# A transformer block with split fp32 products: which engine adds the output projection's results, and when the heads' sums are rounded

## The chip, the cores and the metric

The kernel runs on one core of a Trainium2 chip. A core has TensorE (PE, matrix products, results in PSUM), VectorE (DVE), ScalarE (ACT), GpSimd (POOL) and SyncE (SP, which issues most transfers). Each works through its own queue in order; semaphores order the engines among themselves. In this kernel POOL works on SBUF alone; a product's result that it adds is copied from PSUM to SBUF first. The metric is the time of one execution on the device in microseconds.

## The reference

One block of a hybrid model on 512 tokens of width 1024, all in fp32:

```
n = rmsnorm(x);  proj = n @ w_in
y_gla = gated linear attention, 4 heads, forward and backward
y_mla = softmax attention with latent q and kv, 8 heads, 512 x 512 scores each
merged = sigmoid(z_ma) * y_gla + sigmoid(z_mb) * y_mla
h = x + merged @ w_out
h = h + square(relu(rmsnorm(h) @ w_ff1)) @ w_ff2
out = rmsnorm(h)
```

The change touches the stretch from the softmax attention over `merged @ w_out` to the normalisation in front of the MLP.

## The kernel before

**Split products.** An fp32 operand is kept as two tiles, a rounded high part and the remainder. ACT writes the high part (`split`, line 93) and another engine, VectorE if nothing else is said, subtracts it from the source (line 94). A product is three matmuls: high by high, low by high, high by low (`mm3`, lines 88 to 90).

**Seven products.** The large products with 1024 x 1024 weights are cut into 2 x 2 blocks and done with seven block products in place of eight, on sums and differences of blocks. The left operand of products 1 and 2 are first blocks of `merged` themselves (`split_first`), of 5, 6, 7 and 3 sums of its blocks (`merged_sums` makes the tiles y and z, `split_sum` splits them), of 4 the last block (`corner`). The right operand comes from four weight blocks B11, B12, B21, B22. `load_w2` loads one by four transfers that SP issues; `load_onto` adds another block onto it in SBUF by two accumulating transfers from POOL's queue; `add_w2` adds on VectorE; `split_part` splits one half of a block (tiles bo50h, bo50l for product 5, half 0), `split_w2` both. The split halves share four buffers, so a half can be split when the half four before it has been used.

**The attention loop** (line 1244) runs 38 steps. Step n makes the scores of one head and 128 queries (`att_scores`: product, row maximum on VectorE, exponential on ACT, scaling on ACT or VectorE in turn), transposes those of step n - 3 (`att_flip`, split by ACT and VectorE) and, in every second step, multiplies two steps' probabilities by the values, six steps late (`att_values`). When a head is done, VectorE gates it and POOL adds it to the other branch (`merge`, line 1055). Two heads make a pair p of `merged`. At the end of the steps 13, 21 and 29 the sums of pairs 0, 1 and 2 are made on POOL (lines 928 to 931) and split at once: ACT rounds, POOL takes the remainder. The loop also holds the output weights' loads (steps 26 and 30), the splits of products 1 and 2 (28 and 31), and the first blocks of pairs 0 and 1 (26). In this loop a planner sets the order on ACT, VectorE and TensorE, from the order of the text as priority and from dependencies; POOL follows the text (line 1531). `goes_behind` adds an edge: the first instruction of one stretch behind the last of another on the same engine.

**The projection** (lines 1454 to 1530) runs the products in the order 1, 2, 5, 6, 3, 7, 4, on TensorE, ACT and VectorE in the order of the text (line 1530). Products 1, 6, 7 and 4 accumulate on top of each other in two PSUM banks (`xs_`), 5 and 3 in two others (`zs_`); what is in a bank after one product must be added to the residual rows before the next product goes on. `add_rows` does that on VectorE from PSUM; `add_rows_by_copy` copies on ACT (line 1293) and adds on POOL (line 1295). `normed` squares, scales and so normalises a row block, and `flipped` transposes it on TensorE and splits it for the MLP. Products 3, 7 and 4 run row block by row block.

Of the kernel before, what the change touches and what calls it, by code (L numbers as in the profile page):

```python
# [14 lines left out]
AF = mybir.ActivationFunctionType  # L15
ALU = mybir.AluOpType
# [3 lines left out]
S = 512  # L20
# [36 lines left out]
def tile_block(ctx: ExitStack, tc: tile.TileContext, t, out: bass.AP):  # L57
    nc = tc.nc
# [9 lines left out]
    def u2(name, dt=F32, shape=(P, S)):  # L68
        return tl(list(shape), dt, "u2", 29, name)
# [37 lines left out]
    def traced():  # L107
        return len(nc.cur_bb.bb.instructions)
# [810 lines left out]
    def split_w2(x, name):  # L919
        return [split_part(x, g, name) for g in range(NP // 2)]  # L920
# [24 lines left out]
    def up_units(pr):  # L945

        wq = stage(3, P, f"wq{pr}")
        for k in range(3):
            nc.sync.dma_start(
                wq[:, k, :].rearrange("p (h e) -> p h e", h=2), w_uq[:, k, 2 * pr : 2 * pr + 2, 0:NOPE]  # L950
            )
        wqh, wql = halves(3, P, f"wq{pr}")
        split(wqh, wql, wq, nc.gpsimd)
        wk = stage(2, 384, f"wk{pr}")
        nc.sync.dma_start(
            wk.rearrange("p k (h e) -> p k h e", h=2), w_ukv[:, :, 2 * pr : 2 * pr + 2, :]
        )
        wh, wl = halves(2, 384, f"wk{pr}")
        src = wk.rearrange("p k (h e) -> p k h e", h=2)
        for k in range(2):  # L960
            for c, e in ((slice(0, 128), slice(0, NOPE)), (slice(128, 384), slice(NOPE, 192))):
                split(wh[:, k, c].rearrange("p (h e) -> p h e", h=2),
                      wl[:, k, c].rearrange("p (h e) -> p h e", h=2), src[:, k, :, e], nc.gpsimd)
        qs = []
        for i in range(2):
            q = u4(f"q{pr}{i}")
            h = (2 * pr + i) * HALF
            for x in range(2):
                at = NOPE + x * HALF
                nc.sync.dma_start(raw(q[at : at + HALF]), raw(ro[x][h : h + HALF]))  # L970
            qs.append(q)
        yield
        accq = up_T(wqh, wql, cq, f"uq{pr}")
        for i in range(2):
            split_scaled(qs[i][0:64, 0, :], qs[i][0:64, 1, :], accq[i * 64 : i * 64 + 64, :], QK_SCALE)
        yield
        acck = up_T(wh[:, :, 0:128], wl[:, :, 0:128], ckv, f"uk{pr}")
        for i in range(2):
            kb = kbuf[2 * (pr % 2) + i]
            split(kb[0:64, 0, :], kb[0:64, 1, :], acck[i * 64 : i * 64 + 64, :])  # L980
        yield
        vs = []
        for j in range(2):
            acc = ps("mm", f"uv{pr}{j}")
            for i in range(2):
                tok = slice((2 * j + i) * P, (2 * j + i + 1) * P)
                for k in range(2):
                    mm3(acc[:, i * 256 : i * 256 + 256], ckv[k][:, 0, tok], ckv[k][:, 1, tok],
                        wh[:, k, 128:384], wl[:, k, 128:384], k == 0, k == 1)
            hl = u4(f"v{pr}{j}", F32R, (P, 2, 2, 256))  # L990
            flat = [hl[:, x].rearrange("p a b -> p (a b)") for x in range(2)]
            split_scaled(*flat, acc, 0.5)
            vs.append(hl)
            yield
        for i in range(2):
            heads[2 * pr + i] = (qs[i], kbuf[2 * (pr % 2) + i], vs, slice(i * MV, (i + 1) * MV))
# [244 lines left out]
    LAG_B, LAG_C = 3, 6  # L1241
    units = iter(())
    attending = traced()
    for n in range(4 * MH + LAG_C):
        if n % 8 == 1 and n // 8 + 1 < MH // 2:
            units = up_units(n // 8 + 1)
        if n < 4 * MH:
            att_scores(n // 4, n % 4)
        next(units, None)
        b = n - LAG_B  # L1250
        if 0 <= b < 4 * MH:
            flips = traced()
            att_flip(b // 4, b % 4)
            if b == 0:
                gla_turn(GH - 1, (flips, traced()))
        if n == 26:
            load_w2(0, B11, w_out)
            load_w2(0, B21, w_out)
            for p in range(2):
                split_first(wo_left[p], merged[p][0], f"o{p}", nc.gpsimd)  # L1260
        if n == 28:
            wo_right[1] = split_w2(B11, "bo1")
        if n == 29:
            load_onto(B11, B12, w_out)
        c = n - LAG_C
        if c >= 0 and c % 2 == 1:
            att_values(c // 4, (c % 4) // 2)
        if c > 0 and c % 8 == 7 and c // 8 < NP - 1:
            p = c // 8
            y, z = merged_sums(p, nc.gpsimd)  # L1270
            split_sum(wo_left[p], y, 5, 6, f"bo{p}", nc.gpsimd)
            split_sum(wo_left[p], z, 7, 3, f"co{p}", nc.gpsimd)
        if n == 30:
            load_w2(0, B12, w_out)
            load_w2(0, B22, w_out)
        if n == 31:
            wo_right[2] = split_w2(B21, "bo2")

    hrow = []
    for i in range(NT):  # L1280
# [6 lines left out]
    def add_rows(i, c, acc, op=ALU.add):  # L1287
        hc = hrow[i][:, c * S : (c + 1) * S]
        nc.vector.tensor_tensor(hc, hc, acc, op=op)  # L1289

    def add_rows_by_copy(i, c, acc, sign=1.0):
        part = u2(f"part{i}{c}")
        nc.scalar.activation(part, acc, AF.Copy, scale=sign)
        hc = hrow[i][:, c * S : (c + 1) * S]
        nc.gpsimd.tensor_tensor(hc, hc, part, op=ALU.add)

    ms_rows = {}

# [172 lines left out]
    split_first(wo_left[2], merged[2][0], "o2", nc.vector)  # L1471
    g_last = split_first(wo_left[last], merged[last][0], f"o{last}", nc.vector, None, slice(0, HT))
    wo_product(1)
    split_first(wo_left[last], merged[last][0], f"o{last}", nc.vector, g_last, slice(HT, S))
    wo_right[5] = [split_part(B11, 0, "bo5")]
    y, z = merged_sums(last, nc.vector)
    split_sum(wo_left[last], y, 5, 6, f"bo{last}")
    for rb in range(2):
        add_rows_by_copy(rb, 0, xs_[rb])
    load_onto(B12, B22, w_out)  # L1480
    wo_right[5].append(split_part(B11, 1, "bo5"))
    wo_product(2)
    add_w2(B11, B22, B11, ALU.add)
    for rb in range(2):
        add_rows(rb, 0, ws_[rb])
        first_half_square(rb, 0)
    wo_right[6] = split_w2(B11, "bo6")
    load_onto(B11, B21, w_out)
    load_w2(0, B21)
    wo_product(5)  # L1490
    split_sum(wo_left[last], z, 7, 3, f"co{last}")
    for rb in range(2):
        add_rows_by_copy(2 + rb, 1, zs_[rb])
    wo_right[3] = split_w2(B22, "bo3")
    load_w2(0, B22)
    for p in range(NP):
        corner(p, nc.gpsimd if p < last else nc.vector)
    wo_product(6)
    fm = Flipped(gvec[:, V_MLP : V_MLP + 8], "m")
    mT = fm.out  # L1500
    for rb in range(2):
        add_rows_by_copy(rb, 1, xs_[rb], -1.0)
    wo_right[7] = split_w2(B12, "bo7")
    load_w2(0, B12)
    for rb in range(2):
        wo_product(3, (rb,))
        add_rows(rb, 1, zs_[rb])
        normed(rb, 1)
    wo_right[4] = split_w2(B11, "bo4")
    load_w2(0, B11)  # L1510
    early = [proj_begin(w1, 0, "f00", "at")]
    for rb in range(2):
# [92 lines left out]
```

## Time and profile before

| | |
|---|---|
| median of 3 runs | 790.49 us (789.77 to 790.68) |
| profiled execution | 790.3 us, span 788.6 us |
| TensorE busy | 759.9 us |
| VectorE busy | 587.2 us |
| ScalarE busy | 456.4 us |
| GpSimd busy | 157.2 us |
| mean granted TensorE clock | 0.989 |

Times in the views count from the span's start. A timeline row has the start, the time taken, the engine, the line, the operation, the tile written and those read, the shape, the number of instructions, and in brackets how long the engine had stood idle before and what released it. A row of waits has the sum, the number of times and the longest. In a table of windows the clock that TensorE was granted stands as PEclk (1.00 is full).

### The profile page before, as it was taken

Reading aid. Unit: us, or ns where it says so; the run is one execution under the profiler, and the core shown is the slowest. Engines: PE = TensorE matmul, PEld = TensorE weight load, DVE = VectorE, ACT = ScalarE, POOL = GpSimd, SP = SyncE. Lnnn points to the kernel's source line nnn. Section 1 sums busy time; section 2 is a strip of 40 time slices with the busy share of each in tenths; the row PEclk is TensorE's granted clock in tenths of the full one; section 3 lists DMA queues with packets and bytes.
Section 4 is the critical chain, followed back from the end, with each engine's and each line's share of the span. In section 5 each row is a group of like instructions: output and inputs, shape, how many; then the busy total and the mean of one; then the engine's idle time right before and its main releaser. Section 6 shows DMA issues by size and latency. Waiting matters only on the chain.

```text
span 788.6 us, 10218 instructions
## 1 busy us (share of the span) xinstructions
PE 759.9 (96%) x3744; PEld 641.1 (81%) x3744; DVE 587.2 (74%) x857; ACT 456.4 (58%) x774; POOL 157.2 (20%) x233
## 2 busy tenths in 40 slices
PE   9999999999999999988697999999999999999996
PEld 7888788888888889877585888888888888888885
DVE  7688999576568676977768668875788487857695
ACT  8456666546485556876735676444653456436644
POOL 0710007062452032054734100000000000000014
PEclk9999999999999999999988999999999999999999
DMA  9734201132225233025637441055105511550002
GB/s 311 236 108 141 78 2 46 37 81 80 54 54 140 44 84 94 1 68 180 156 108 154 139 119 55 25 190 154 33 27 187 160 30 51 160 171 18 27 1 106
DMA packets 94945, 77.09 MB, mean 98 GB/s; under 512 B 15312, under 2 KB 74704, under 8 KB 94896
## 3 DMA queue, kind: packets, MB, share of 16 engines
q1 hardware_dynamic: 92752, 72.24, 31.1%
q0 software_dynamic: 1856, 3.93, 2.7%
q8 instruction: 29, 0.48, 0.3%
q10 hardware_dynamic: 288, 0.28, 0.1%
q14 instruction: 20, 0.16, 0.1%
HBM read 72.76 MB, written 2.10 MB: 95 GB/s over the span
## 4 chain that ended last, share of the span: by engine, by line
PE 84%; issue 5%; DVE 4%; POOL 3%; ACT 3%; POOLq 0%; DVEq 0%; ACTq 0%
PE f L89 7%; PE f L90 7%; PE f L88 7%; PE gx L88 4%; PE gx L90 4%; PE gx L89 4%; PE first L326 3%; PE za L88 2%; PE za L90 2%; PE za L89 2%; PE gz L88 2%; PE gz L90 2%; PE gz L89 2%; PE zb L88 1%; PE zb L90 1%
## 5 line engine op out<-in xcount | busy, mean ns | idle before, releaser
L1544 POOL DMA_DIRECT2D gfin<-in_g_final x1 | 0.6, 645 | 283.2 <-PE f L90 283.2
L912 DVE TENSOR_TENSOR w<-w,w 128x1024 f32<-128x1024 f32 x34 | 41.1, 1219 | 0.3
L474 POOL COPY v3f<-rrf 128x4 f32<-128x4 f32 x4 | 2.8, 708 | 135.8 <-DVE rrf L457 135.8
L1024 PE MATMUL tp<-ident,e 128*128 128x128 f32 x128 | 20.0, 283 | 7.4 <-ACT e L1015 5.7
L1024 PEld LDWEIGHTS tp<-ident,e 128*128 128x128 f32 x128 | 16.0, 145 | 10.6 <-ACT e L1015 5.9
L1010 ACT ACTIVATE e<-s,top 128x512 f32<-128x512 f32 x32 | 21.9, 684 | 3.9 <-DVE top L1007 3.7
L94 DVE TENSOR_TENSOR pT<-tp,pT 128x512 fp32r<-128x512 f32 x32 | 21.6, 682 | 1.9 <-ACT pT L93 1.8
L1289 DVE TENSOR_TENSOR h<-h,gx 128x512 f32<-128x512 f32 x32 | 21.5, 680 | 1.9 <-PE gx L90 1.8
L1007 DVE TENSOR_REDUCE top<-s 128x1 f32<-128x512 f32 x32 | 21.6, 679 | 1.1 <-PE s L90 1.0
L93 ACT ACTIVATE pT<-tp 128x512 fp32r<-128x512 f32 x32 | 18.8, 594 | 4.3 <-PE tp L1024 4.1
L88 PE MATMUL av<-pT,v 128*128 128x256 f32 x64 | 19.8, 309 | 0.0
L89 PE MATMUL av<-pT,v 128*128 128x256 f32 x64 | 19.1, 299 | 0.0
L90 PE MATMUL av<-pT,v 128*128 128x256 f32 x64 | 18.5, 290 | 0.0
L1367 ACT ACTIVATE fa<-f 128x512 f32<-128x512 f32 x32 | 18.5, 577 | 0.0
L88 PE MATMUL s<-kbuf,q 96*128 96x512 f32 x32 | 13.9, 434 | 4.7 <-ACT e L1010 4.7
L93 ACT ACTIVATE ghb<-y 128x512 fp32r<-128x512 f32 x16 | 10.1, 632 | 14.0 <-DVE y L859 14.0
L94 DVE TENSOR_TENSOR sc<-sc,sc 128x512 fp32r<-128x512 f32 x16 | 10.9, 690 | 9.5 <-ACT sc L93 9.5
L1055 POOL TENSOR_TENSOR mx<-tb,za 128x256 f32<-128x256 f32 x8 | 6.5, 816 | 50.0 <-DVE tb L1052 50.0
L93 ACT ACTIVATE sc<-sc 128x512 fp32r<-128x512 f32 x16 | 9.3, 595 | 11.5 <-DVE sc L545 11.5
L173 ACT ACTIVATE ms<-h 128x512 f32<-128x512 f32 x8 | 5.0, 628 | 18.7 <-DVE h L1289 18.7
L93 ACT ACTIVATE b_00h<-w 128x1024 fp32r<-128x1024 f32 x7 | 7.4, 1060 | 12.6 <-PE gz L90 6.0
L93 ACT ACTIVATE b_10h<-w 128x1024 fp32r<-128x1024 f32 x7 | 7.4, 1060 | 12.1 <-PE gz L90 6.0
(1643 smaller groups left out, 2961.2 us busy)
## 6 DMA issues: line engine op xcount, KB each, us to landing
w<-in_w_ff SPq DMA_DIRECT2D x64, 256.0 KB, 3.5
grw<-in_w_in SPq DMA_DIRECT2D x8, 512.0 KB, 9.2
gvw<-in_w_in SPq DMA_DIRECT2D x8, 512.0 KB, 4.7
w<-in_w_out SPq DMA_DIRECT2D x16, 256.0 KB, 3.6
w<-in_w_out POOLq DMA_DIRECT2D x6, 512.0 KB, 6.8
x<-in_xt SPq DMA_DIRECT2D x8, 256.0 KB, 5.2
vw<-in_w_first SPq DMA_DIRECT2D x8, 256.0 KB, 5.3
h<-in_x SPq DMA_DIRECT2D x4, 512.0 KB, 7.5
```

Of the source, the lines that this page charges most:

```text
L88: nc.tensor.matmul(acc, lh, rh, start=start, stop=False, skip_group_check=onto)
L89: nc.tensor.matmul(acc, lh, rl, start=False, stop=False, skip_group_check=onto)
L90: nc.tensor.matmul(acc, ll, rh, start=False, stop=stop, skip_group_check=onto)
L93: nc.scalar.activation(hi, src, AF.Copy)
L94: rest.tensor_tensor(lo, src, raw(hi), op=ALU.subtract)
L326: nc.tensor.matmul(f_accs[i], a[:, i * P : (i + 1) * P], b, start=k == 0 and x == 0, stop=k == KD - 1 and x == 2)
L912: nc.vector.tensor_tensor(wq[dst][g], wq[x][g], wq[y][g], op=op)
L1007: nc.vector.tensor_reduce(top, acc, axis=AX.X, op=ALU.max, negate=True)
L1010: nc.scalar.activation(e, acc, AF.Exp, bias=top, accum_out=tot)
L1024: nc.tensor.transpose(tp[:, k * P : (k + 1) * P], e[:, k * P : (k + 1) * P], ident)
L1289: nc.vector.tensor_tensor(hc, hc, acc, op=op)
L1367: nc.scalar.activation(a, acc, AF.Relu)
```

## The change

In the projection the six additions that went by ACT's copy and POOL become `add_rows` on VectorE, the second with a subtraction in place of a negated copy; the remainders of the last block for pairs 0, 1 and 2 go from POOL to VectorE. The splits of weight halves are put between these additions: half 0 of a block before them, half 1 behind; the halves of product 4 stand inside the loop over row blocks, each behind `normed`. The accumulating load of B22 onto B12 and the sum for product 6 come before the additions of product 1, and the split of the last pair's z before product 5.

In the attention loop the sums of pairs 0, 1 and 2 are made where they were, but split at steps 17, 25 and 31, and on ACT behind that step's scores. The first blocks of pairs 0 and 1 are split at step 25. The loads of B11 and B21 stand at step 20 (26 before), the splits of products 1 and 2 at 24 and 27 (28 and 31), the load of B12 onto B11 at 28 (29).

```diff
+    sums_of = {}
     for n in range(4 * MH + LAG_C):
...
+        scored = traced()
         if n < 4 * MH:
             att_scores(n // 4, n % 4)
+        scored = scored, traced()
...
-        if n == 26:
+
+        ready = traced()
+        if n in (17, 25, 31):
+            p = (n - 13) // 8
+            y, z = sums_of.pop(p)
+            split_sum(wo_left[p], y, 5, 6, f"bo{p}", nc.gpsimd)
+            split_sum(wo_left[p], z, 7, 3, f"co{p}", nc.gpsimd)
+            if p == 1:
+                for p in range(2):
+                    split_first(wo_left[p], merged[p][0], f"o{p}", nc.gpsimd)
+            goes_behind((ready, traced()), scored, SPLITTERS[:1])
+        if n == 20:
             load_w2(0, B11, w_out)
             load_w2(0, B21, w_out)
-            for p in range(2):
-                split_first(wo_left[p], merged[p][0], f"o{p}", nc.gpsimd)
+        if n == 24:
+            wo_right[1] = split_w2(B11, "bo1")
+        if n == 27:
+            wo_right[2] = split_w2(B21, "bo2")
         if n == 28:
-            wo_right[1] = split_w2(B11, "bo1")
-        if n == 29:
             load_onto(B11, B12, w_out)
+        if n == 30:
+            load_w2(0, B12, w_out)
+            load_w2(0, B22, w_out)
         c = n - LAG_C
         if c >= 0 and c % 2 == 1:
             att_values(c // 4, (c % 4) // 2)
         if c > 0 and c % 8 == 7 and c // 8 < NP - 1:
-            p = c // 8
-            y, z = merged_sums(p, nc.gpsimd)
-            split_sum(wo_left[p], y, 5, 6, f"bo{p}", nc.gpsimd)
-            split_sum(wo_left[p], z, 7, 3, f"co{p}", nc.gpsimd)
-        if n == 30:
-            load_w2(0, B12, w_out)
-            load_w2(0, B22, w_out)
-        if n == 31:
-            wo_right[2] = split_w2(B21, "bo2")
+            sums_of[c // 8] = merged_sums(c // 8, nc.gpsimd)
...
     wo_product(1)
+    wo_right[5] = [split_part(B11, 0, "bo5")]
     split_first(wo_left[last], merged[last][0], f"o{last}", nc.vector, g_last, slice(HT, S))
-    wo_right[5] = [split_part(B11, 0, "bo5")]
     y, z = merged_sums(last, nc.vector)
     split_sum(wo_left[last], y, 5, 6, f"bo{last}")
+    wo_right[5].append(split_part(B11, 1, "bo5"))
+    load_onto(B12, B22, w_out)
+    add_w2(B11, B22, B11, ALU.add)
     for rb in range(2):
-        add_rows_by_copy(rb, 0, xs_[rb])
-    load_onto(B12, B22, w_out)
-    wo_right[5].append(split_part(B11, 1, "bo5"))
+        add_rows(rb, 0, xs_[rb])
     wo_product(2)
-    add_w2(B11, B22, B11, ALU.add)
+    wo_right[6] = [split_part(B11, 0, "bo6")]
     for rb in range(2):
         add_rows(rb, 0, ws_[rb])
         first_half_square(rb, 0)
-    wo_right[6] = split_w2(B11, "bo6")
+    wo_right[6].append(split_part(B11, 1, "bo6"))
     load_onto(B11, B21, w_out)
     load_w2(0, B21)
+    split_sum(wo_left[last], z, 7, 3, f"co{last}")
     wo_product(5)
-    split_sum(wo_left[last], z, 7, 3, f"co{last}")
+    wo_right[3] = [split_part(B22, 0, "bo3")]
     for rb in range(2):
-        add_rows_by_copy(2 + rb, 1, zs_[rb])
-    wo_right[3] = split_w2(B22, "bo3")
+        add_rows(2 + rb, 1, zs_[rb])
+    wo_right[3].append(split_part(B22, 1, "bo3"))
     load_w2(0, B22)
     for p in range(NP):
-        corner(p, nc.gpsimd if p < last else nc.vector)
+        corner(p, nc.vector)
     wo_product(6)
...
+    wo_right[7] = [split_part(B12, 0, "bo7")]
     for rb in range(2):
-        add_rows_by_copy(rb, 1, xs_[rb], -1.0)
-    wo_right[7] = split_w2(B12, "bo7")
+        add_rows(rb, 1, xs_[rb], ALU.subtract)
+    wo_right[7].append(split_part(B12, 1, "bo7"))
     load_w2(0, B12)
     for rb in range(2):
         wo_product(3, (rb,))
         add_rows(rb, 1, zs_[rb])
         normed(rb, 1)
-    wo_right[4] = split_w2(B11, "bo4")
+        wo_right.setdefault(4, []).append(split_part(B11, rb, "bo4"))
```

More of the change, by code (lines that the diff above doesn't have):

```diff
@@ L1289, in add_rows @@
         nc.vector.tensor_tensor(hc, hc, acc, op=op)
[L1291 to L1295, printed above, removed]
     ms_rows = {}
```

## The prediction

> **What bounds the kernel now.** I read the page first, then TensorE's waits, then a table of windows over the second half of the attention and the projection (the stages that the change touches), and last the timeline of each engine around the waits.
>
> ```profile
> span 788.6 us, 10218 instructions
> PE 759.9 (96%) x3744; PEld 641.1 (81%) x3744; DVE 587.2 (74%) x857; ACT 456.4 (58%) x774; POOL 157.2 (20%) x233
> ```
> ```profile
> PE tp L1024 <- ACT e L1015: 5.7, 1, 5.7
> PE woz L89 <- DVE bo30l L94: 5.1, 1, 5.1
> PE s L88 <- ACT e L1010: 4.7, 2, 2.5
> ```
> ```profile
> core 0: us, PE busy (x) PEld busy (x) DVE busy (x) ACT busy (x) POOL busy (x), PEclk, DMA share, GB/s
> 369.60:395.60 26.00, 18.62 (x121) 16.49 (x122) 21.01 (x39) 20.32 (x41) 18.03 (x17) 0.94 0.61 160
> 395.60:405.60 10.00, 10.00 (x50) 8.63 (x49) 5.31 (x9) 2.90 (x5) 1.86 (x2) 0.82 0.35 137
> 405.60:436.00 30.40, 24.57 (x97) 19.52 (x96) 24.03 (x21) 14.32 (x26) 15.35 (x16) 0.89 0.62 136
> 444.50:788.60 344.10, 336.33 (x1540) 279.37 (x1540) 247.42 (x336) 180.24 (x295) 13.40 (x17) 0.99 0.30 90
> ```
>
> TensorE is busy for 96% of the span, so time can only be won where it stands still or runs at a reduced clock. Its large waits all lie between 342 and 445 us: 4.7 + 5.7 us in the attention loop, 5.1 us in the projection and, in a row below, 1.1 us behind it. Behind 444.5 us it is 98% busy, so what is won before that should reach the end. The granted clock (PEclk) falls too: (1-0.94) x 2 x 26.0 + (1-0.82) x 2 x 10.0 = 6.7 us at half rate around 395 us, and (1-0.89) x 2 x 30.4 = 6.7 us in the projection; each follows a wait of over 5 us.
>
> ```profile
> 343.02 0.63 ACT L93 ACTIVATE ghbo<-yo 128x512 fp32r<-128x512 f32 x1 [1.60 <-POOL yo L929]
> ...
> 369.59 0.50 PE L88 MATMUL s<-kbuf,q 96*128 96x512 f32 x1 [2.46 <-ACT e L1010]
> 377.01 1.05 ACT L93 ACTIVATE bo10h<-w 128x1024 fp32r<-128x1024 f32 x1
> 385.82 1.53 DVE L94 TENSOR_TENSOR bo20l<-w,bo20h 128x1024 fp32r<-128x1024 f32 x1
> 386.34 1.61 POOL L928 TENSOR_TENSOR yo<-my 128x256 f32<-128x256 f32 x1
> 387.28 1.75 DVE L94 TENSOR_TENSOR bo21l<-w,bo21h 128x1024 fp32r<-128x1024 f32 x1
> 389.65 0.63 ACT L93 ACTIVATE ghbo<-yo 128x512 fp32r<-128x512 f32 x1 [3.83 <-POOL yo L929]
> 393.65 1.97 PE L1024 MATMUL tp<-ident,e 128*128 128x128 f32 x8 [5.73 <-ACT e L1015]
> ```
>
> The timeline shows what ACT waits for before those stalls: the rounding of a pair's sum (ghbo) stands in ACT's queue until POOL has the sum, and the exponentials behind it, which TensorE needs, wait too. This happens three times; the last is longest because VectorE and POOL slow each other (1.53, 1.75 and 1.61 us).
>
> ```profile
> 405.58 0.39 PE L88 MATMUL wow<-bo20h,gao 128*128 128x512 f32 x1
> 422.91 0.39 PE L88 MATMUL woz<-bo30h,ghco 128*128 128x512 f32 x1
> 442.39 1.03 PE L198 MATMUL mb<-ident,ms 128*128 128x128 f32 x8
> 444.52 0.47 PE L88 MATMUL wox<-bo40h,gdo 128*128 128x512 f32 x1 [1.10 <-DVE h L1289]
> ```
> ```profile
> 408.80 2.26 DVE L94 TENSOR_TENSOR bo51l<-w,bo51h 128x1024 fp32r<-128x1024 f32 x1 [1.23 <-ACT bo51h L93]
> 413.25 1.27 DVE L1289 TENSOR_TENSOR h<-h,wow 128x512 f32<-128x512 f32 x2
> 416.28 1.23 DVE L94 TENSOR_TENSOR bo60l<-w,bo60h 128x1024 fp32r<-128x1024 f32 x1 [1.76 <-ACT bo60h L93]
> 417.42 1.22 DVE L94 TENSOR_TENSOR bo61l<-w,bo61h 128x1024 fp32r<-128x1024 f32 x1
> 419.65 8.73 DVE L94 TENSOR_TENSOR bo30l<-w,bo30h 128x1024 fp32r<-128x1024 f32 x1 [0.41 <-ACT bo30h L93]
> 429.44 0.41 DVE L94 TENSOR_TENSOR gdo<-my,gdo 128x256 fp32r<-128x256 f32 x1
> 436.28 0.68 DVE L1289 TENSOR_TENSOR h<-h,woz 128x512 f32<-128x512 f32 x1
> 443.70 1.27 DVE L1289 TENSOR_TENSOR h<-h,wox 128x512 f32<-128x512 f32 x2
> ```
> ```profile
> 418.57 1.05 ACT L93 ACTIVATE bo30h<-w 128x1024 fp32r<-128x1024 f32 x1
> 419.52 1.05 ACT L93 ACTIVATE bo31h<-w 128x1024 fp32r<-128x1024 f32 x1
> 438.58 0.72 ACT L1312 ACTIVATE ms<-h,hp 128x512 f32<-128x512 f32 x1 [0.86 <-POOL hp L183]
> 419.70 3.12 POOL L1295 TENSOR_TENSOR h<-h,part 128x512 f32<-128x512 f32 x2
> ...
> 424.28 3.00 POOL L1295 TENSOR_TENSOR h<-h,part 128x512 f32<-128x512 f32 x2
> ```
>
> In the projection, the remainder bo30l took 8.73 us where its neighbour took 1.22: it began as POOL's run of additions and corner remainders began (419.70) and ended one op's length after that run (424.28 + 3.00 = 427.28). TensorE stood 5.1 us for it and then worked at half rate.
>
> **Part 1: projection additions and remainders on VectorE.** Removed: six copies on ACT (ACT is busy 14.3 of 30.4 us there, so they are worth nothing in themselves), six POOL additions and three POOL remainders. Added to VectorE: six additions at 0.6 us (two in 1.27) and three corner remainders at about 0.4, or 3.6 + 1.2 = 4.8 us. Gone: the stretch of bo30l (8.73 - 1.22 = 7.5) and of bo51l (2.26 - 1.22 = 1.0). VectorE's 24.0 us of this window become 24.0 - 8.5 + 4.8 = 20.3, against TensorE's four products at (422.91 - 405.58 - 0.7 of waiting) / 3 = 5.5 us, or 22 us. So VectorE is nearly the bound, and its order must be followed. In microseconds after product 1's end (405.58), with 1.15 for a remainder (start to start) and 0.95 for ACT's half of it: bo51l ends at 3.5, the sum of weight blocks (two of 1.15) 5.8, two additions 7.0, bo60l 8.1, two additions 9.3; ACT squares two rows before bo61h, so bo61l ends at 12.2, the last pair's z remainder 12.8, bo30l 14.0, two additions 15.2, bo31l 16.3, four corners 17.7, bo70l 18.9, two additions 20.1, bo71l 21.2. TensorE wants block 6 at 11.0, its second half at 13.7, block 3 at 16.5, block 7 at 22.0: all in time, so the waits of 5.1 and 0.7 us and the half-rate stretch go.
>
> What is late next comes from the edit that splits block 4 inside the row loop. Product 3 of the first row block ends at 19.3, but VectorE is free for its addition only at 21.2. Addition to normalised row takes 436.28 to 438.58 + 0.72, or 3.0 us: 24.2. Then ACT rounds bo40 (25.2), VectorE takes its remainder (26.3), and only then comes the second row block's addition, which was in front of block 4 before: normalised at 29.3, bo41 31.4, the first MLP remainder 32.5, the next addition and with it product 4 at about 33.3. TensorE, through product 7 and the first transposes (1.0 us each) at 28.3, waits 1.0 us for the second normalised rows and 3.0 us for that addition, in place of 1.1. Product 4 begins 33.3 us after product 1's end; now 444.52 - 405.58 = 38.9. **Gain 5.6 us.** Bounds: 9.8 if VectorE's order never binds (two half products and two transposes after 22.0 put product 4 at 29.1); 3.2 if the wait of 3.0 us brings a reduced clock again, which would cost half of 6.7 us less the 1.0 or so of slack that TensorE has in its next waits.
>
> **Part 2: sums rounded four steps later.** The rounding goes behind the exponential of its step on ACT, four steps on (two for the last pair), when POOL should long have the sums. POOL keeps its work and its order; its additions of the next head now stand behind a rounding, but have four steps until their own sums. The first stall (4.7 - 2.5 = about 2.2) and the second (2.46) should go; each split still takes ACT 1.3 us in its new place, where TensorE is at full load. I take 2.0 for each, between 0 (the stall only moves) and the whole. The third stall is mixed. From 369.6 to 395.6 us ACT has 20.3 us of work and VectorE 21.0, so the 26.0 cannot fall below 21. The change moves the same roundings from its end to its middle; with about 1.5 us for filling and draining I take 22.5, a gain of 3.5, and 0.5 for the half-rate tail behind 395.6, where TensorE also waits for the last heads. Together 4.0, between 0 and 5.0 + 1.8 (all of the tail).
>
> **Part 3: first weights sooner.** Four loads per block are issued earlier by program order and the splits of blocks 1 and 2 come four steps sooner. No load is seen to hold the first split (bo10h at 377.01 has no wait in front), so the loads are worth nothing.
>
> ```profile
> 355.53 18.43 SPq L902 DMA_DIRECT2D w<-in_w_out x16
> 387.38 1.69 SPq L902 DMA_DIRECT2D w<-in_w_ff x2
> ```
>
> The sync queue has a free stretch from the last of the sixteen issues (373.96) to 387.38, so nothing behind them is delayed. POOL's two accumulating loads of block 5 move one step ahead, in front of the last merges that feed the third pair; those of block 7 no longer stand behind additions. I take 0 for both: the splits' 1.15 us on VectorE and 0.95 on ACT are counted in the 21 us above.
>
> **Sum.** 2.0 + 2.0 + 4.0 + 5.6 = 13.6 us from the profiled execution's 790.3 (its span and 1.7 around it): 776.7. The median of the runs is 790.49, 0.2 above the profiled execution: 777.
>
> [...] The traced row is a TensorE wait of 2.46 us without a lower clock behind it and one of 5.1 with one. [...] The row bo30l stood for POOL's whole run of instructions. [...]
>
> **Rivals.** (a) The attention stalls only move, because ACT and VectorE are the bound around the last two pairs: the first stall goes and the rest stays: 790.5 - 2.0 - 5.6 = 783. For it: 20.3 and 21.0 of 26.0 us busy. Against: 5.7 us of TensorE's waiting lies directly behind one wait of ACT. (b) All stalls go and VectorE keeps up: 790.5 - 2.2 - 2.5 - 6.8 - 9.8 = 769. Against it: VectorE's order above. (c) Slower. POOL's run in the loop (two remainders of sums and two first blocks at step 25) now meets VectorE's remainders of bo10, bo11 (step 24) and bo20, bo21 (step 27), the same kind of op as bo30l. Each one caught as bo30l was costs 7.5 us, with scores and transposes queued behind it, and 3.4 us of reduced clock: 10.9. One caught leaves a gain of 3; from two on it decides: 776.7 + 21.8 = 798. For it: bo30l. Against: bo20l and bo21l lost only 0.3 and 0.5 us beside POOL's sums. (d) The change doesn't do what it says: the planner sets the order of ACT in the loop, and could leave a rounding waiting on POOL as now, while VectorE's new 4.8 us eat the rest: 790.
>
> **How the numbers follow.** Forecast 0.60; (a) 0.20; (b) 0.07; (c) 0.08; (d) 0.05, of which I put 0.03 within 0.2% (1.6 us, about what a measurement tells from no change) and 0.02 beyond it on the slow side. So faster 0.87, same 0.03, slower 0.10. The forecast's own range is 772 to 782; with (a), (b) and one op caught in (c) it is 769 to 787.
>
> **What would show it.** Part 1: bo30l near 1.2 us, no TensorE wait for it, PEclk 1.00 in that window, a wait of about 3 us for h in front of product 4, which starts some 33 us after product 2's first matmul. Part 2: no ACT wait for yo before an exponential, TensorE's waits on e below 3 us in all. Part 3: bo10h earlier by some steps with no effect of its own. The prediction would be wrong by VectorE remainders far over 1.3 us in the loop, by ACT waiting on POOL at the last pair, or by a reduced clock before product 4.

## The result and the profile after

The changed kernel takes 777.11 us (median of four runs, 776.68 to 777.62) against 790.48 us: a ratio of 0.983, 95% interval 0.982 to 0.985. The forecast was 777.0. The profiled execution has a span of 775.3 us (788.6 before). First the page's engine line and the rows of TensorE's waits (sum, times, longest).

```profile
span 775.3 us, 10210 instructions
PE 757.8 (98%) x3744; PEld 640.1 (83%) x3744; DVE 584.6 (75%) x866; ACT 452.9 (58%) x768; POOL 148.9 (19%) x224
```
```profile
PE s L88 <- DVE pT L94: 3.2, 2, 2.7
PE wox L88 <- DVE h L1298: 3.1, 1, 3.1
...
PE av L88 <- ACT pT L93: 1.3, 1, 1.3
PE mb L198 <- DVE ms L1314: 1.2, 1, 1.2
```

The waits on `e` (4.7 + 5.7 us) and on bo30l (5.1 us) are gone. In their place stand 3.2 + 1.3 us in the attention loop and 1.2 + 3.1 us in the projection. The table of windows is cut at about the same work as the one of before: the last heads in the loop, products 2 to 3 with the first half of 7, the place where product 4 waits, and the rest.

```profile
core 0: us, PE busy (x) PEld busy (x) DVE busy (x) ACT busy (x) POOL busy (x), PEclk, DMA share, GB/s
...
363.00:387.00 24.00, 19.61 (x117) 17.20 (x118) 21.53 (x39) 17.75 (x40) 17.24 (x17) 0.86 0.57 169
...
397.20:422.10 24.90, 24.90 (x114) 20.64 (x114) 20.44 (x30) 12.64 (x21) 3.36 (x5) 1.00 0.72 166
422.10:430.60 8.50, 4.29 (x24) 3.20 (x22) 5.43 (x8) 3.69 (x6) 0.56 (x1) 0.88 0.24 86
430.60:775.30 344.70, 338.05 (x1540) 280.97 (x1540) 247.70 (x336) 180.25 (x295) 13.38 (x17) 0.99 0.30 90
```

From 397.2 to 422.1 us TensorE has no idle time at all, at full clock, with VectorE busy for 20.44 us. All that is left in the projection lies in the 8.5 us behind that. In the loop VectorE is busy for 21.53 of 24.0 us, and the clock falls (0.86 is 6.7 us at half rate).

The first matmul of product 2, the last wait and the start of product 4 give the division of the gain; the VectorE rows below them are those that the prediction followed one by one.

```profile
397.01 0.39 PE L88 MATMUL wow<-bo20h,gao 128*128 128x512 f32 x1
426.47 1.09 PE L198 MATMUL mb<-ident,ms 128*128 128x128 f32 x8 [1.18 <-DVE ms L1314]
430.64 0.79 PE L88 MATMUL wox<-bo40h,gdo 128*128 128x512 f32 x1 [3.08 <-DVE h L1298]
```
```profile
410.12 1.21 DVE L94 TENSOR_TENSOR bo30l<-w,bo30h 128x1024 fp32r<-128x1024 f32 x1
...
417.26 1.21 DVE L94 TENSOR_TENSOR bo71l<-w,bo71h 128x1024 fp32r<-128x1024 f32 x1
...
422.49 1.23 DVE L94 TENSOR_TENSOR bo40l<-w,bo40h 128x1024 fp32r<-128x1024 f32 x1 [1.21 <-ACT bo40h L93]
...
427.63 1.22 DVE L94 TENSOR_TENSOR bo41l<-w,bo41h 128x1024 fp32r<-128x1024 f32 x1 [1.22 <-ACT bo41h L93]
...
429.91 1.27 DVE L1298 TENSOR_TENSOR h<-h,wox 128x512 f32<-128x512 f32 x2
```

Up to product 2 the kernel gains 405.58 - 397.01 = 8.6 us. From product 2 to product 4 it takes 430.64 - 397.01 = 33.6 us in place of 38.9, a gain of 5.3. Behind product 4's start it loses 344.7 - 344.1 = 0.6. Together 13.3, the difference of the spans.

In the loop the roundings of the sums (ghbo) no longer wait for POOL, but the third stall has left a remainder. Rows of ACT, POOL, VectorE and TensorE around it:

```profile
346.50 0.63 ACT L93 ACTIVATE ghbo<-yo 128x512 fp32r<-128x512 f32 x1
...
370.31 0.63 ACT L93 ACTIVATE ghbo<-yo 128x512 fp32r<-128x512 f32 x1
...
371.35 0.63 ACT L93 ACTIVATE ghco<-zo 128x512 fp32r<-128x512 f32 x1
371.87 1.08 ACT L93 ACTIVATE pT<-tp 128x512 fp32r<-128x512 f32 x2
...
376.20 0.69 ACT L1010 ACTIVATE e<-s,top 128x512 f32<-128x512 f32 x1 [2.59 <-DVE top L1007]
```
```profile
371.01 1.47 POOL L94 TENSOR_TENSOR glbo<-yo,ghbo 128x512 fp32r<-128x512 f32 x1 [4.86 <-ACT ghbo L93]
372.45 2.24 POOL L94 TENSOR_TENSOR glco<-zo,ghco 128x512 fp32r<-128x512 f32 x1
374.65 2.69 POOL L94 TENSOR_TENSOR gao<-mx,gao 128x512 fp32r<-128x512 f32 x2
```
```profile
370.15 1.21 DVE L94 TENSOR_TENSOR bo20l<-w,bo20h 128x1024 fp32r<-128x1024 f32 x1
...
371.36 2.21 DVE L94 TENSOR_TENSOR bo21l<-w,bo21h 128x1024 fp32r<-128x1024 f32 x1
373.49 1.48 DVE L1013 TENSOR_SCALAR e<-e,tot 128x512 f32<-128x512 f32 x1
374.89 0.68 DVE L94 TENSOR_TENSOR pT<-tp,pT 128x512 fp32r<-128x512 f32 x1
```
```profile
372.51 0.38 PE L88 MATMUL av<-pT,v 128*128 128x256 f32 x1 [1.35 <-ACT pT L93]
375.62 0.79 PE L88 MATMUL s<-kbuf,q 96*128 96x512 f32 x1 [2.73 <-DVE pT L94]
```

The two waits of TensorE there have different causes. The first, 1.35 us, is for ACT, which does the roundings of step 25 one behind another before it comes to the transposed probabilities (pT at 371.87). The second, 2.73 us, is for VectorE. POOL's run of remainders (371.0 to 377.3) meets VectorE's bo21l, which takes 1.0 us more than bo20l just before it, and a scaling, which takes 1.48 us. The remainder of pT and the next row maximum stand behind these; TensorE waits for the first of them, and ACT 2.59 us for the second.

### The profile page after: what moved, and what is told of

Its sections match the earlier page's. It is cut to its first block, busy times and chain, and to the rows that moved or that the text cites. A ratio compares the mean times of both kernels' runs of the same rounds, so it can differ in the third digit from the quotient of the medians.

```text
span 775.3 us, 10210 instructions
## 1 busy us (share of the span) xinstructions
PE 757.8 (98%) x3744; PEld 640.1 (83%) x3744; DVE 584.6 (75%) x866; ACT 452.9 (58%) x768; POOL 148.9 (19%) x224
## 4 chain that ended last, share of the span: by engine, by line
PE 93%; DVE 4%; issue 1%; ACT 1%; POOL 0%; POOLq 0%; DVEq 0%; ACTq 0%
PE f L89 8%; PE f L90 8%; PE f L88 8%; PE gx L88 4%; PE gx L89 4%; PE gx L90 4%; PE first L326 3%; PE za L88 2%; PE za L89 2%; PE za L90 2%; PE gz L89 2%; PE gz L90 2%; PE gz L88 2%; PE tp L1024 2%; PE zb L88 1%; PE zb L90 1%
## 5 line engine op out<-in xcount | busy, mean ns | idle before, releaser
L1298 DVE TENSOR_TENSOR h<-h,gx 128x512 f32<-128x512 f32 x32 | 21.5, 680 | 1.9 <-PE gx L90 1.8
L94 DVE TENSOR_TENSOR pT<-tp,pT 128x512 fp32r<-128x512 f32 x32 | 21.5, 679 | 0.4 <-ACT pT L93 0.2
L93 ACT ACTIVATE b_20h<-w 128x1024 fp32r<-128x1024 f32 x7 | 7.4, 1060 | 11.9 <-PE gz L90 6.0
```

Source lines behind the costliest of these rows:

```text
L93: nc.scalar.activation(hi, src, AF.Copy)
L94: rest.tensor_tensor(lo, src, raw(hi), op=ALU.subtract)
```

## The experiments

Each run is given as a ratio to the kernel before on the same chip, and the trace of each is divided at the same places. In the table "to 2" is the start of product 2, "2 to 4" the time from there to the start of product 4, "4 to f" from there to the first matmul of the MLP, "rest" from there to the end of the span (all us, profiled execution).

| kernel | ratio (95%) | median | to 2 | 2 to 4 | 4 to f | rest |
|---|---|---|---|---|---|---|
| before | 1 | 790.48 | 405.6 | 38.9 | 5.6 | 338.5 |
| after | 0.983 (0.982 to 0.985) | 777.11 | 397.0 | 33.6 | 7.8 | 336.9 |
| loop_alone | 0.989 (0.987 to 0.990) | 782.42 | 397.9 | 39.2 | 5.6 | 338.5 |
| projection_alone | 0.994 (0.992 to 0.996) | 787.32 | 406.8 | 33.7 | 7.6 | 336.9 |
| engines_undone | 0.986 (0.984 to 0.988) | 779.97 | 397.6 | 36.4 | 5.6 | 338.6 |
| engines_alone | 0.990 (0.988 to 0.992) | 783.87 | 406.7 | 31.8 | 7.0 | 337.1 |
| corners_alone | 0.995 (0.993 to 0.997) | 787.54 | 405.4 | 36.2 | 5.5 | 338.6 |
| block4_behind | 0.981 (0.980 to 0.983) | 776.80 | 397.6 | 32.4 | 8.4 | 336.8 |
| late_sums_alone | 0.982 (0.979 to 0.984) | 776.62 | 396.5 | 33.6 | 7.9 | 336.9 |
| run_parted | 0.981 (0.979 to 0.982) | 776.14 | 397.2 | 33.6 | 6.9 | 337.3 |
| both_parts_old_order | 0.979 (0.977 to 0.981) | 774.17 | 397.1 | 31.8 | 5.5 | 338.6 |
| f00_behind_addition | 0.982 (0.980 to 0.984) | 777.26 | 396.7 | 30.6 | 6.3 | 342.7 |
| z_behind_block3 | one run | 790.47 | 405.7 | 39.0 | 5.5 | 338.6 |
| transfer_behind | one run | 792.36 (before: 793.0) | 408.4 | 38.2 | 7.0 | 337.2 |

**The two halves.** Each half of the diff was put into the kernel before by itself: the loop's text of the changed kernel in loop_alone, all of the projection's in projection_alone.

```diff
 loop_alone: the attention loop as changed, the projection as before
+        if n in (17, 25, 31):
+            p = (n - 13) // 8
...
 projection_alone: the attention loop as before, the projection as changed
-        add_rows_by_copy(rb, 0, xs_[rb])
+        add_rows(rb, 0, xs_[rb])
...
```


> The attention loop of the changed kernel with the projection of the one before. Theory (the loop wins by taking ACT's waits for POOL's sums away, independently of the projection): product 2 begins 8.6 us sooner, as in the changed kernel (397.0 against 405.6), bo30l stays near 8.7 us and TensorE waits about 5 us for it; time 790.5 - 8.6 = 782. Rival (the two parts need each other, because POOL's work left in the projection delays something of the loop): less than 5 us won, 786 or more.

> The loop of the kernel before with the projection of the changed one. Theory: from product 2's first matmul to product 4's 33.6 us in place of 38.9, the loop's three waits unchanged, about 0.6 us lost again behind product 4 as in the changed kernel; time 790.5 - 5.3 + 0.6 = 785.8. Rival (the whole gain is in the loop, the projection only trades one wait for another): within 1.6 us of 790.5.

Measured: 0.9886 and 0.994. Their product is 0.983, the ratio of the whole change, so the halves add up. loop_alone has the old projection to the letter: bo30l takes 8.73 us and TensorE waits 5.1 us for it. The loop's part is worth 9 us, the projection's 4 to 5. In projection_alone product 2 starts 1.2 us later than before, although the text up to product 1 is the same; the last section shows from engines_alone, which has that text too, how the clock does this.

**What in the projection.** The changed kernel with the old engines in the new order (engines_undone), the old order with the new engines (engines_alone), and the kernel before with only the three corner remainders moved (corners_alone):

```diff
 engines_undone, against after (the same for the other additions)
-        add_rows(rb, 0, xs_[rb])
+        add_rows_by_copy(rb, 0, xs_[rb])
...
-        corner(p, nc.vector)
+        corner(p, nc.gpsimd if p < last else nc.vector)
```
```diff
 engines_alone, against before (the same for the other additions)
-        add_rows_by_copy(rb, 0, xs_[rb])
+        add_rows(rb, 0, xs_[rb])
...
 engines_alone and corners_alone, against before
-        corner(p, nc.gpsimd if p < last else nc.vector)
+        corner(p, nc.vector)
```


> The changed kernel with its order of the projection, but the six additions again by ACT's copy and POOL, and three corner remainders again on POOL. Theory (VectorE is held while POOL runs): a VectorE remainder in this window is stretched to over 4 us again, TensorE waits for it; 4 to 8 us slower than the changed kernel, 781 to 785. Rival (the new order alone is what helps, VectorE now having more time before each product): no VectorE remainder over 2.5 us and no more than 1.6 us slower; with 4.8 us less work on VectorE perhaps faster than 777.

> The kernel before with the six additions and three corner remainders on VectorE, everything else in its old order and the loop as before. Theory (POOL's run is what held bo30l): bo30l falls to 1.2 us, TensorE's 5.1 us wait and the reduced clock behind it go, product 2 to product 4 falls from 38.9 by 4 to 6 us; time 785 to 787. Rival (the order is what counts; with 4.8 us more work on VectorE in the old order every product waits a little): TensorE waits for three or more different remainders or additions, product 2 to product 4 above 36 us; time 787 to 791.

> The kernel before with only the three corner remainders moved from POOL to VectorE, so that POOL's run beside bo30l is two additions, a gap, two additions. Theory (a VectorE op is held until POOL has nothing ready): bo30l ends in the gap, about 3.1 + 1.2 = 4.3 us long, TensorE waits some 1 us for it, 786 or so. Rival (it is held until the last of the additions whatever stands between): still over 7 us, within 1.6 us of before. Rival (it is held for one POOL instruction at a time): under 2.6 us.

In engines_undone no VectorE instruction is held long, although POOL has all its old work back. VectorE's rows of its timeline:

```profile
411.75 1.22 DVE L94 TENSOR_TENSOR bo30l<-w,bo30h 128x1024 fp32r<-128x1024 f32 x1
413.39 1.82 DVE L94 TENSOR_TENSOR bo31l<-w,bo31h 128x1024 fp32r<-128x1024 f32 x1 [0.42 <-ACT bo31h L93]
...
416.56 1.76 DVE L94 TENSOR_TENSOR bo70l<-w,bo70h 128x1024 fp32r<-128x1024 f32 x1
```

The three remainders beside POOL's run that stand here lose at most 0.6 us each, and two of POOL's additions there take 4.05 us where the next two take 2.52. The expectation of a hold of over 4 us fell: the new order is enough to break it. Product 4 still starts only 36.4 us after product 2, since POOL's additions come late (VectorE waits 1.86 us for one of them).

In engines_alone bo30l takes 1.22 us too, in the old order. So either of the two edits frees it. And product 4 comes 1.9 us earlier after product 2 than with the new order (31.8 against 33.7 in projection_alone, which has the same loop): the new order costs time once VectorE has the work. From product 2 to product 4 the engines alone win 7.2 us, the order alone 2.8 (engines_undone against loop_alone), both together 5.3. In corners_alone POOL's run has a gap where the corners were, and bo30l is let go there, after 4.26 us. VectorE's row, then POOL's:

```profile
419.41 4.26 DVE L94 TENSOR_TENSOR bo30l<-w,bo30h 128x1024 fp32r<-128x1024 f32 x1 [0.42 <-ACT bo30h L93]
```
```profile
419.46 3.12 POOL L1295 TENSOR_TENSOR h<-h,part 128x512 f32<-128x512 f32 x2
422.90 4.16 POOL L1295 TENSOR_TENSOR h<-h,part 128x512 f32<-128x512 f32 x2 [0.32 <-ACT part L1293]
```

The first two additions end at 422.58 us, and bo30l 1.1 us later.

**The step that the prediction called late next.** block4_behind is the changed kernel with block 4 split behind both normalised rows, as before:

```diff
-        wo_right.setdefault(4, []).append(split_part(B11, rb, "bo4"))
+    wo_right[4] = split_w2(B11, "bo4")
     load_w2(0, B11)
```


> The changed kernel with both halves of block 4 split behind both normalised row blocks, as before. Theory (block 4's first half in front of the second row block's addition causes the 3.1 us wait before product 4): that wait shrinks by about 1.2 us to 1.9, the 1.2 us wait for ms goes, the granted clock stays full there; 0.5 to 1.5 us faster than the changed kernel, about 776. Rival (VectorE's total work in the projection sets the wait, wherever block 4 stands): product 4 begins within 0.3 us of the changed kernel's 33.6 us behind product 2, time the same.

Product 4 comes 1.2 us sooner (32.4), and TensorE's wait for ms is gone. So some 1.2 of the 1.9 us that the new order costs come from this one place. But the wait in front of product 4 becomes 3.3 us, where some 1.9 was expected, and the half clock that comes in it has only 0.8 us of the wait in it (2.1 in the changed kernel) and lies on work for the rest: 8.4 us from the start of product 4 to the MLP, against 7.8. Of the 1.2 us the end keeps some 0.6 in the profiled execution; against the whole kernel that is within what two intervals can tell apart.

**What in the loop.** late_sums_alone takes the changed kernel and puts the loads, the splits of blocks 1 and 2 and the first blocks back at their old steps (the accumulating load too); only the sums stay late. run_parted puts the sums of pair 1 two steps sooner, and the first blocks of pairs 0 and 1 apart, so that POOL's run at step 25 falls into pieces.

```diff
 late_sums_alone, against after
-        if n == 20:
+        if n == 26:
             load_w2(0, B11, w_out)
             load_w2(0, B21, w_out)
+            for p in range(2):
+                split_first(wo_left[p], merged[p][0], f"o{p}", nc.gpsimd)
-        if n == 24:
+        if n == 28:
             wo_right[1] = split_w2(B11, "bo1")
-        if n == 27:
+        if n == 31:
             wo_right[2] = split_w2(B21, "bo2")
...
 run_parted, against after
-        if n in (17, 25, 31):
+        if n in (17, 23, 31):
...
-            if p == 1:
-                for p in range(2):
-                    split_first(wo_left[p], merged[p][0], f"o{p}", nc.gpsimd)
+            if p < 2:
+                split_first(wo_left[p], merged[p][0], f"o{p}", nc.gpsimd)
```


> The changed kernel with only the sums split later: the loads, the splits of products 1 and 2, the first blocks of pairs 0 and 1 and the accumulating load at their old steps (26, 28, 31, 26, 29). Theory (ACT's wait for POOL's sums is the cause, the weights are worth nothing): within 1.6 us of the changed kernel's 777.1. Rival (weights split earlier free the last score steps from the splits of product 2, which is where the 5.7 us wait got its length): 2 to 4 us slower, with a TensorE wait of over 3 us for a row maximum or an exponential of the last scores.

> The changed kernel with pair 1's sums split at step 23 in place of 25, and the first block of pair 0 at step 17, of pair 1 at 23. In the changed kernel POOL idles from 366.2 to 371.0 us and then runs four remainders beside VectorE's bo20l, bo21l and a scaling, which take 1.2, 2.2 and 1.5 us; TensorE waits 1.3 + 2.7 us there and drops to half rate for 6.8 us. Theory (the remaining wait of the loop is the meeting of these two runs): TensorE's waits in the loop fall below 2.5 us, no reduced clock in the loop, 2 to 4 us faster than 777.1. Rival (VectorE and ACT are full there in any order): waits of about 4 us at another place, time within 1.6 us.

late_sums_alone measures the same as the whole change (776.62 against 777.11 us, the intervals overlap): the weights sooner are worth nothing that these intervals can tell. Whether the sums win by the later step or by their place behind the scores on ACT was not tried apart. late_sums_alone has no meeting of bo21l and POOL's run, and yet waits in other places: TensorE waits 2.2 us for a pT and 2.0 us for an e, both from VectorE, and 0.5 us in two short waits. The waits in run_parted (a fifth is 0.3 us):

```profile
PE s L88 <- ACT e L1010: 2.0, 2, 1.4
...
PE tp L1024 <- ACT e L1015: 0.7, 1, 0.7
PE wox L88 <- DVE pT L94: 0.6, 1, 0.6
PE tp L1024 <- DVE pT L94: 0.5, 1, 0.5
```

In three different orders TensorE waits 4.5, 4.7 and some 4.1 us in this stretch. That the order hardly matters speaks for the work itself as what remains of the third stall: VectorE's 21.5 of 24.0 us. No run took work away from VectorE there, so this is not shown. run_parted may win 1 us; its interval overlaps that of the changed kernel. Its expected end of the waits and of the reduced clock in the loop did not come: the clock still falls there, for 3.4 us.

**What holds bo30l.** Two edits of the kernel before look for the condition. In z_behind_block3 the split of the last pair's z goes behind that of block 3, so that bo30l starts ahead of POOL's run and not with it. In transfer_behind POOL's two accumulating transfers onto B11 are issued behind two of its additions and the corner remainders, so that these no longer follow the transfers.

```diff
 z_behind_block3, against before
-    split_sum(wo_left[last], z, 7, 3, f"co{last}")
     for rb in range(2):
         add_rows_by_copy(2 + rb, 1, zs_[rb])
     wo_right[3] = split_w2(B22, "bo3")
+    split_sum(wo_left[last], z, 7, 3, f"co{last}")
...
 transfer_behind, against before
-    load_onto(B11, B21, w_out)
     load_w2(0, B21)
     wo_product(5)
...
         corner(p, nc.gpsimd if p < last else nc.vector)
+    load_onto(B11, B21, w_out)
     wo_product(6)
```


> The kernel before with the split of the last pair's z behind those of block 3, so that bo30l starts about 0.6 us in front of POOL's run and not 0.05 us. Theory (the long hold needs both to start together; a VectorE op that is under way when POOL starts takes turns with POOL, as in engines_undone): bo30l under 2 us, TensorE's 5.1 us wait gone. Rival (any VectorE op with two SBUF inputs in front of a POOL run with all inputs ready is held for the whole run): bo30l over 6 us again.

> The kernel before with POOL's two accumulating transfers onto B11 issued behind its first two additions and three corner remainders, so that nothing but additions and remainders runs on POOL beside VectorE's glco and bo30l. Theory (the transfers issued right in front of POOL's run have to do with the long hold): no VectorE op over 2.6 us there, ops of both engines take turns, TensorE's 5.1 us wait gone, span about 785. Rival (the run of ready POOL ops alone holds VectorE): a VectorE op there takes over 4 us again, span within 1.6 us of 788.6.

First POOL's transfers and additions and VectorE's bo30l in z_behind_block3, then the same engines in transfer_behind:

```profile
417.93 2.46 POOL L908 DMA_DIRECT2D w<-in_w_out  x2 [2.23 <-DVE bo60l L94]
419.84 3.13 POOL L1295 TENSOR_TENSOR h<-h,part 128x512 f32<-128x512 f32 x2
...
419.27 9.26 DVE L94 TENSOR_TENSOR bo30l<-w,bo30h 128x1024 fp32r<-128x1024 f32 x1 [0.49 <-ACT bo30h L93]
```
```profile
428.47 2.44 POOL L908 DMA_DIRECT2D w<-in_w_out  x2
430.03 3.44 POOL L1295 TENSOR_TENSOR h<-h,part 128x512 f32<-128x512 f32 x2
...
423.05 2.32 DVE L94 TENSOR_TENSOR bo30l<-w,bo30h 128x1024 fp32r<-128x1024 f32 x1
...
429.53 5.03 DVE L94 TENSOR_TENSOR bo71l<-w,bo71h 128x1024 fp32r<-128x1024 f32 x1
```

A start of 0.57 us ahead of the run doesn't help: bo30l is held for 9.26 us. A simultaneous start is not the condition. With the transfers behind, bo30l takes 2.32 us beside POOL's run, and the hold moves with the transfers: bo71l, beside the two additions issued right behind them, takes 5.03 us. That is why the expected time of about 785 us did not come. So in these traces the hold goes with a run of POOL work issued straight behind two transfers. That is not the whole condition. In engines_undone POOL's second transfer came 2.2 us after the first (409.36 and 411.54), additions stood right behind it too, and nothing was held. Which part of this matters was not tried further.

**The better order.** both_parts_old_order joins the projection of engines_alone with the loop of late_sums_alone. f00_behind_addition then moves the remainder of the first MLP weights, which stands in front of the additions that product 4 waits for, behind the first of these.

```diff
 f00_behind_addition, against both_parts_old_order
-    early = [proj_begin(w1, 0, "f00", "at")]
+    early = []
...
         first_half_square(2 + rb, 1)
+        if rb == 0:
+            early.append(proj_begin(w1, 0, "f00", "at"))
```


> The old order of the projection with its additions and remainders on VectorE, and the loop with the sums split later and the weights at their old steps. Theory (the new order of the projection costs what engines_alone, 31.75 us from product 2 to product 4, won over projection_alone, 33.65; the loop's part is late_sums_alone's): product 2 at 396.5, product 4 at 428.2, span 396.5 + (782.5 - 406.7) = 772.3; some 774 us, 2.5 to 3 faster than the changed kernel. Rival (the reduced clock falls on other work when the loop ends sooner and takes the gain): 776 or more.

> The same with the split of the first MLP weights put behind product 7's first addition. Theory (VectorE's queue in front of that addition is what product 4 waits for): the 2.6 us wait before product 4 falls by 1.1 to about 1.5 and the clock stays full there; 1 to 2 us faster than both_parts_old_order. Rival (VectorE's whole work up to the normalised rows is the bound, in whatever order): product 4 earlier, the first MLP product not; the same within 0.5 us.

both_parts_old_order takes 774.17 us, 0.979 (0.977 to 0.981): better than the kernel before and, by some 3 us, than the changed one, whose interval just misses it. From product 2 on the profiled executions differ by 2.4 us: 1.9 by which product 4 comes sooner, the rest because its wait of 2.6 us did not lower the clock, which the last section puts down to where it fell. Counted from product 2, f00_behind_addition starts product 4 another 1.1 us sooner and the MLP only 0.4 us; it then loses 4.1 us in the rest, where waits for normalised rows (1.06 and 1.54 us) now fall close together and the clock is lower (0.8 in the page's slice from 427 to 446 us). But the profiled execution is one of the longest of its four: they took 774.65 to 778.02 us, the first of these at a mean clock of 0.998, the second at 0.992. So the clock's loss does not come each time, and the best of them only equals both_parts_old_order. That fits VectorE's work up to the MLP as the bound, whose order only moves the wait; no run took work away to show it.

## Why the prediction was right, and where it wasn't

The total was right (777.0 against 777.1), and so were its larger terms. That it came within 0.1 us is luck: 0.6 us lost behind product 4 and 0.6 won at the start of the span, neither of them in the sum, cancel.

*Part 1, the projection: 5.6 predicted, 5.3 measured.* VectorE's order, followed instruction by instruction, came out: bo30l ended 14.3 us after product 2's first matmul (14.0 predicted), bo71l 21.5 (21.2), product 4 started at 33.6 (33.3). VectorE's 20.3 us for the stage were 20.44. The two new waits, 1.0 and 3.0 us, were 1.18 and 3.08, and each at the named place. In terms of the account: the projection's waits fell from 5.1 + 1.1 + 0.7 to 3.1 + 1.2, or 2.6 us, and the half-rate stretch from 426.4 to 433.3 us, which cost (6.8 - 2.0 of waiting inside it) / 2 = 2.4 us, left this place.

*The reduced clock.* The forecast left it out and kept it for the lower bound. It came, 0.9 us after that wait's start. The bound took half of 6.7 us less 1.0 of slack, about 2.4. Up to the first matmul of the MLP it cost 2.2 (7.8 against 5.6) and not 3.35, because 2.1 us of the stretch at half rate lay on the wait itself. Behind that 1.6 came back (336.9 against 338.5) and not 1.0; two waits of 0.6 us each at the MLP's start, in the trace of before, are gone. The net 0.6 is the loss behind product 4. Both terms of the bound were mis-sized.

*Part 2, the loop: 8.0 predicted, 8.6 measured, of which 0.6 is no work of the change.* The first product of scores already starts at 303.85 us in place of 304.46, with the same text up to there: four of the first matmuls (tile `first`, line 326) take 1.30 us in place of 1.91. So the column "to 2" holds 0.6 us between these two traces that no edit made. Both first stalls went whole, where 2.0 of each was taken. The third was predicted to end at 22.5 us for 21 of work. It kept 4.1 us of waiting, and the clock fell there instead of at product 1. By waits: 4.7 + 5.7 + 0.9 + 0.7 before, 3.2 + 1.3 after, 7.5 fewer; beside the 0.6, some 0.5 is left that I can't tie to a row. The floor that the prediction read from 20.3 and 21.0 us of ACT and VectorE fits what three orders of the loop ran into.

*Rival (c), the one with the other sign,* came true in small. POOL's run at step 25 did meet bo21l, but cost it 1.0 us, not 7.5, and the scaling behind it about as much. It lost less there than either of the two remainders that POOL had beside it takes (1.47 and 2.24 us); the 8.73 us of bo30l and the 5.03 of bo71l are longer than any one POOL instruction beside them (the additions there take 3.12 and 3.44 us for two).

*Part 3: 0 predicted, nothing measured* (late_sums_alone).

*The step that failed* is in Part 1, "gone: the stretch of bo30l", which was credited to the move from POOL to VectorE, and in rival (c), which took the hold for something that any VectorE remainder meets beside any POOL run. engines_undone shows that the order alone ends it, transfer_behind that it follows two transfers back to back. The sum did not suffer, because the change had both edits. The other miss is one of omission. The prediction named the split of block 4 inside the row loop as what is late next, and priced it rightly as part of the 33.3, but didn't ask what the change would be without the new order. engines_alone, block4_behind and both_parts_old_order answer: 1.9 us between products 2 and 4, of which 1.2 for the split in the row loop, and some 3 us in time.

## What to carry to other kernels

When work moves to an engine with an in-order queue, write that queue out instruction by instruction with the durations of the trace; here that put product 4 within 0.3 us. Then ask of each edit whether the others need it: the engines alone took 7.2 us off the projection up to product 4, and with the interleaving that came with them it was 5.3. Where one instruction takes several times its usual length, find the condition by moving one neighbour at a time before the stretch is counted as a property of the engines.

## What the runs showed of the hardware

**In these traces the half-rate stretches of the clock lie on a grid of 3.41 us, and a wait of the same length came with one or without.** In the kernel before they start at 392.3 and 426.4 us (34.1 us apart, 10 of 3.41), in the changed kernel at 373.9 and 428.5 (54.6 us, 16 of 3.41). Each of these four lasts two units, 6.8 us; the one at 345.9 in engines_alone lasts one, 3.4 us. Cut on that grid, the table of windows shows what stood ahead of them. First the same wait of 2.26 us in the loop, in the kernel before and in engines_alone, whose text is the same up to there:

```profile
341.10:344.51 3.41, 2.38 (x18) 2.00 (x16) 1.98 (x3) 1.07 (x3) 3.25 (x6) 1.00 0.16 28
344.51:347.92 3.41, 2.18 (x15) 2.04 (x16) 1.66 (x5) 3.41 (x9) 3.41 (x3) 1.00 0.01 2
```
```profile
342.52:345.93 3.41, 1.15 (x8) 0.86 (x6) 0.84 (x3) 2.67 (x7) 3.41 (x4) 1.00 0.01 1
345.93:349.35 3.42, 3.42 (x18) 3.31 (x17) 1.92 (x5) 1.91 (x5) 3.42 (x6) 0.50 0.10 28
```

Before, the wait is shared by two units, each has over 2.1 us of matmuls, and the clock stays at 1.00. In engines_alone it falls into one, which has 1.15 us, and the next unit runs at half rate. The waits in front of product 4, in the changed kernel and in both_parts_old_order:

```profile
425.09:428.50 3.41, 1.30 (x9) 0.86 (x8) 1.51 (x3) 2.57 (x3) 0.56 (x1) 1.00 0.39 135
428.50:431.92 3.42, 1.27 (x3) 1.08 (x4) 2.69 (x4) 1.34 (x6) 0.18 (x1) 0.50 0.47 168
431.92:435.33 3.41, 3.41 (x9) 2.64 (x9) 2.98 (x8) 3.41 (x10) 0.19 (x1) 0.50 0.49 139
```
```profile
423.53:426.94 3.41, 2.65 (x16) 2.06 (x14) 2.38 (x3) 2.89 (x4) 0.00 (x0) 1.00 0.03 10
426.94:430.35 3.41, 1.55 (x7) 1.33 (x8) 2.31 (x3) 1.67 (x6) 0.37 (x2) 1.00 0.90 287
430.35:433.76 3.41, 3.41 (x17) 2.83 (x16) 3.23 (x8) 3.41 (x9) 0.00 (x0) 1.00 0.55 167
```

From 313 to 450 us, the four full-rate units that such a stretch followed in the kernel before and in the changed kernel had 3.42, 3.13, 2.34 and 2.11 us of idle time; no other full-rate unit of these two traces had more than 1.26. In engines_alone 2.26 us was followed by half rate and in projection_alone 1.91 us (434.64 to 438.06), while the 1.86 us in both_parts_old_order was not. Each of the four stretches ended behind its second unit, which had no idle time (the first had 1.35 to 2.15 us); the one at 345.9 in engines_alone ended behind its first, which had none. So the same wait of 2.26 us came with 3.4 us at half rate, 1.7 us of clock, in one trace and with none in the other; what the windows show to differ is where it lay on the grid. The 2.11 us ahead of the changed kernel's second stretch are of two waits: all of the 1.2 us in front of product 4, and the first 0.9 of the 3.1. What sets the place of the grid, no run shows.

**A VectorE remainder of a weight half (128x1024) was held over a whole run of POOL instructions**: for 8.73 us in the kernel before and 9.26 in z_behind_block3, both ending 1.1 us after the run; for 4.26 in corners_alone, where the run has a gap; for 5.03 over two additions in transfer_behind. Each time the run was issued straight behind two accumulating transfers of POOL's queue. Beside other POOL work the same kind of instruction took 1.5 to 2.3 us (1.53 and 1.75 in the kernel before, 2.21 in the changed kernel, 2.32 in transfer_behind). What makes the difference beyond that stays open.
